# Two-layer encoder on one core: other distances in SBUF between the weight tiles and the activation parts

## The chip, the core and the metric

The kernel runs on one core of a Trainium2 chip. Its engines are TensorE (PE, with its weight loads shown apart as PEld), VectorE (DVE), ScalarE (ACT), GpSimd (POOL) and SyncE (SP, which only issues DMAs here). The metric is device time in microseconds of one execution.

## What is computed

An encoder trunk of two layers on 256 tokens of width 1024, all in float32. Each layer is a SwiGLU half-step, a mixer with 16 attention heads, a second SwiGLU half-step and a gate:

```
for i in range(2):
    x = x + 0.5 * swiglu(rms_norm(x, norm_ffn1[i]), ffn1_w_in[i], ffn1_w_out[i])   # 1024 -> 2 x 2816 -> 1024
    h = rms_norm(x, norm_mix[i])
    qa, ka, va, qb, kb, vb = split(h @ w_qkv[i])                 # 8 heads A, 8 query and 2 key heads B, 64 wide
    oa = dilated_attention(norm(qa), norm(ka), va, bias_a)
    ob = banded_attention(norm(qb), norm(kb), vb, 128, bias_b, sink_b[i])
    x = x + concat(oa, ob) @ w_o[i]
    x = x + 0.5 * swiglu(rms_norm(x, norm_ffn2[i]), ffn2_w_in[i], ffn2_w_out[i])
    x = x + sigmoid(rms_norm(x, norm_ple[i]) @ w_ple_gate[i]) * (p[i] @ w_ple_proj[i])
```

## The kernel before, in words

Every float32 operand of a matrix product is split into two parts of type float32r, an upper (h) and a lower (l), and a product is three matmuls into one PSUM bank: upper by upper, upper by lower, lower by upper (`mm3`). The stationary operand (lhsT, loaded into the array) is a 128 x 128 tile of the transposed activations; the moving operand (rhs, streamed through it) is 512 or 256 columns of a weight tile.

The weights come as chunks of 128 x 1024 floats, in one fixed order (class `Weights`). SP's queue loads a chunk into one of four `wraw` buffers; ScalarE writes its upper part `whi`, VectorE its lower part `wlo`, eight buffers each. The next load is issued when a `wraw` buffer is free again.

The activations' parts are: `ah`, `al`, x^T in two parts for each token tile of 128, made by `x_T` for an `Acts` object, one object a stage; they are the stationary operand of the products with w_in, w_qkv and the gate's weights. `pth`, `ptl`, three buffers each from `take_pt`: in a half-step h^T, the transposed block j of 256 hidden columns (11 blocks a half-step), the stationary operand of the product with w_out (`unit_rows`); in the mixer the transposed probabilities, there the moving operand of the product with v. `oth`, `otl`: the heads' outputs and p^T in the mixer, and x^T of the first half-step of all (`first_acts`). Transposes are matmuls with an identity, through the banks `tp` and `op`.

Class `Pace` keeps an expected clock and from it fixes the order in which the program issues instructions on each engine. Addresses don't enter into it.

Tiles lie in SBUF in the order of the pools. Of the start of each tile in a partition the build gives, in bytes past a multiple of 512:

| tile | before | after |
|---|---|---|
| whi, wlo (all buffers; every slice used starts a multiple of 1024 further on) | 480 | 0 |
| ah, al | 480 | 0 plus the stage's shift |
| pth, ptl in the half-steps | 32 | 0 plus the block's shift |
| oth, otl | 32 | 0 |
| qah, qal, kah, kal, qbh, qbl, kbh, kbl | 32 | 0 |
| vah, val, vbh, vbl | 480 | 0 |
| identity | 96 | 128 |

All buffers of one name have the same remainder, and the 128 stationary columns used at a time (512 bytes) begin at multiples of 512 from the tile's start; those of v begin at multiples of 256. So each product has one distance, start of the stationary slice minus start of the weight slice, mod 512: before, 0 for ah and al with whi and wlo, and 64 for pth, ptl, oth and otl with them. For q k it is 0, for the product with v 192 or 448.

Of the kernel before, what the change touches and what calls it, by code (L numbers as in the profile page):

```python
# [32 lines left out]
def shape_constants():  # L33
    """One-hot T5 buckets and additive log-multiplicity masks by position distance 255 - i."""
    d = 255 - np.arange(512)
    n = np.abs(d)
    half, exact = NB // 2, NB // 4
    nf = np.maximum(n, 1).astype(np.float32)
    large = exact + (
        np.log(nf / np.float32(exact)) / np.float32(math.log(MAXD / exact)) * np.float32(half - exact)  # L40
    ).astype(np.int32)
    large = np.minimum(large, half - 1)
    bucket = np.where(d > 0, half, 0) + np.where(n < exact, n, large)
    onehot = (np.arange(NB)[:, None] == bucket[None, :]).astype(np.float32)
    mult = (n <= 64).astype(int) + (d % 4 == 0) + (d % 16 == 0)
    mask_a = np.where(mult > 0, np.log(np.maximum(mult, 1)), NEG)
    mask_b = np.where(n <= 128, 0.0, NEG)
    masks = np.stack([mask_a, mask_b]).astype(np.float32)
    sel = np.zeros((2, NHA + NHB), np.float32)
    sel[0, :NHA] = 1.0  # L50
    sel[1, NHA:] = 1.0
    return onehot, masks, sel
# [5 lines left out]
def column_chunks(w, starts, width):  # L58
    """[D, 1024, N] to chunks [D, starts, chunk, 128, 1024]: the columns from starts on, by feature rows."""
    blocks = [np.concatenate([w[:, :, c:c + width] for c in cols], axis=2) for cols in starts]  # L60
    v = np.stack(blocks, axis=1)
    cw = v.shape[-1]
    v = v.reshape(DEPTH, len(starts), KD * cw // 1024, 1024 // cw, 128, cw)
    return np.ascontiguousarray(v.transpose(0, 1, 2, 4, 3, 5)).reshape(DEPTH, len(starts), -1, 128, 1024)


def lay_out(inputs):
    """The inputs as the kernel loads them: contiguous chunks, token-transposed copies, gains by partition."""
    a = {name: np.ascontiguousarray(v) for name, v in inputs.items()}
    onehot, masks, sel = shape_constants()  # L70
    d = {}
    for name in ("ffn1", "ffn2"):
        starts = [(j * FB, DFF + j * FB) for j in range(NFB)]
        d[name + "_in"] = column_chunks(a[name + "_w_in"], starts, FB)
        d[name + "_out"] = a[name + "_w_out"].reshape(DEPTH, -1, 128, DM)
    d["qkv"] = np.concatenate([column_chunks(a["w_qkv"], [(c0,)], cw)[:, 0] for _, c0, cw in QKV_BLOCKS], axis=1)
    for name, w in (("wo", "w_o"), ("gate", "w_ple_gate"), ("ple", "w_ple_proj")):
        d[name] = a[w].reshape(DEPTH, -1, 128, DM)
    x = a["x"][0].reshape(2, 128, DM)
    d["x"] = x  # L80
    d["xT"] = a["x"][0].T.reshape(4, 2, 128, S).transpose(0, 2, 1, 3)
    d["pT"] = a["p"][:, 0].reshape(DEPTH, S, 2, 128).transpose(0, 3, 2, 1)
    g = [a[n].reshape(DEPTH * KD, 128) for n in ("norm_ffn1", "norm_mix", "norm_ffn2", "norm_ple")]
    g += [np.concatenate([a[n], a[n]], axis=1) for n in ("q_norm_a", "k_norm_a", "q_norm_b", "k_norm_b")]
    d["gains"] = np.concatenate(g).T
    d["sink"] = a["sink_b"].reshape(1, -1)
    d["bias"] = np.concatenate([a["rel_bias"], sel])
    d["distance"] = np.concatenate([onehot, masks])
    return {name: np.ascontiguousarray(v) for name, v in d.items()}


# The start: identities that keep the tensor engine busy, and when the first loads are expected.
# [6 lines left out]
class Pace:  # L99
    """The order in which instructions are issued.  # L100

    Each engine runs its instructions in the order of issue. The tensor engine is the
    busiest, so its expected progress is the clock: work for the other engines is issued
    once what it needs is expected to be there, and never ahead of work that can go first.
    """
# [12 lines left out]
    def done(self):  # L118
        """When the other engines can see what the tensor engine has been given so far."""
        return self.now + self.FROM_PE  # L120
# [13 lines left out]
    def at(self, t, fn, engine=None, prio=0):  # L134
        """fn() from time t on; with an engine: once that is free, the lowest prio first."""
# [3 lines left out]
    def check(self):  # L139
        """Issues what has become due, then weight splitting into the time that is left."""  # L140
# [16 lines left out]
    def until(self, cond):  # L157
        """Nothing else is left for the tensor engine: waits for an event's result."""
# [6 lines left out]
class Weights:  # L165
    """The stream of weight chunks, each [128, 1024] columns, split into two float32r parts.

    Chunks are loaded, split and used in one fixed order; a chunk's slots are free again
    once it has had all its uses.
    """  # L170
# [12 lines left out]
    def add(self, src, pieces, uses=2):  # L183
        """src: [128, 1024] in DRAM; pieces: (start, stop, gain or None)."""
# [16 lines left out]
    def ready(self):  # L201
        """When the next chunk has arrived and its slots are free."""
        return max(self.arrived.get((self.cut, self.at), self.arrived[self.cut]), self.freed.get(self.cut - self.SPLIT, 0.0))

    def piece(self):
        """Up to 512 columns: the upper part now, the lower part when that is expected."""
# [35 lines left out]
    def lows(self, n):  # L242
        """Issues the lower parts up to the n-th; loads what can go into the raw slots then free."""
# [9 lines left out]
    def pump(self):  # L253
        """Splits ahead while the engines for it have nothing more urgent."""
# [27 lines left out]
def encoder(ctx: ExitStack, tc, ins, out):  # L282
# [16 lines left out]
    # A slot is taken again only when all that uses it has been issued: a total order, no deadlock.  # L299
# [16 lines left out]
    def give(tile, t=0.0):  # L316
        """tile's slot can be taken from time t on; all that uses tile has been issued."""
        kind, k, _ = owner.pop(id(tile))
        slots[kind][k] = t
# [8 lines left out]
    def when(kind, fn):  # L328
        """fn() once a slot can be taken."""
# [11 lines left out]
    W = Weights(nc, pace, wraw_p, whi_p, wlo_p)  # L341
    pace.fill = W.pump
    gains = const.tile([P, 72], F32, name="gains")
# [46 lines left out]
    def unit_cols(ps, a, t, ids, c, cw, kks=None):  # L390
        """ps += chunk c's part of the product with token tile t."""
# [13 lines left out]
    def unit_rows(acc, ah, al, c, first, last, ready):  # L405
        """acc[n] += (ah + al)^T (row chunk c) for the two column halves n."""
# [8 lines left out]
    def transposes(kind, blocks, ready=0.0):  # L415
        """blocks: (destination columns / 128, source); on a bank of its own."""
# [7 lines left out]
    def with_bank(kind, t, fn):  # L424
        """fn() from time t on, once the transposes' bank is expected to be free."""
# [7 lines left out]
    def parts(hi, lo, src, n, scale=None, bank=None, then=None, ready=None, prio=1):  # L433
        """hi + lo = src * scale; returns when they are expected. bank: src's, free after that."""
# [28 lines left out]
    x_sb = const.tile([P, 2, DM], F32, name="x_sb")  # L463
    xT_in = [tile_L() for _ in range(4)]
# [25 lines left out]
    # The tensor engine's clock rises once it has been busy: identities until the first data is there.  # L490
# [5 lines left out]
    def setup():  # L496
        """The scales of q k^T, and the position bias by distance, one DRAM row per head."""
# [11 lines left out]
        nc.gpsimd.dma_start(out=bias_d, in_=bs[:16, :])  # L509
        give(bs)  # L510

    # v with zero columns beside it, so that a head's product fills its half of a pair's rows
# [15 lines left out]
    class Acts:  # L528
        def __init__(self, hi=None, lo=None):
            def part(name, given):  # L530
                if given is not None:
                    return [given[:, :, t * P:(t + 1) * P] for t in range(2)]
                return [act_p.tile([P, KD, P], F32R, tag=f"{name}{t}", name=f"{name}{t}") for t in range(2)]
# [5 lines left out]
    def x_T(a, t, ready):  # L539
        """Issues x^T of token tile t when x is expected, each half as soon as it can."""  # L540
# [10 lines left out]
    def stats(a, t):  # L551
        """1/rms of token tile t's rows."""
# [24 lines left out]
    def first_acts():  # L577
        """The parts of x^T and of the first weights, in the order of their loads."""
# [22 lines left out]
    def take_pt():  # L601
        return take("pt", *(att.tile([P, 2, S], F32R, tag=g, name=g, bufs=3) for g in ("pth", "ptl")))
# [6 lines left out]
    def ffn(a, ids, first=False):  # L609
# [27 lines left out]
        def h_T(j, ts, ready):  # L637
            if j not in hT:
                hT[j] = take_pt()
# [73 lines left out]
    def mixers(i, a, d):  # L713
# [13 lines left out]
        def head_T(key, ps, t, nh, perm, scale, dst):  # L727
            """Normed heads, two by two transposed into dst: hi and lo [2 heads' features, pairs, tokens]."""
# [56 lines left out]
        def block(name, kind, cw, evac, split=False):  # L785
            """A generator of the block's units, with evac(ps, t) after a token tile's last."""
# [41 lines left out]
        def qk(h):  # L828
# [23 lines left out]
            def logits():  # L852
                """L = -(q k + bias), nm = -max, or -max with the sink."""
# [79 lines left out]
        def embed():  # L933
            """The two parts of this layer's p^T; they lie where later heads' outputs will."""
            pr = ple[1][:, 512:]
            nc.gpsimd.dma_start(out=pr.rearrange("q (k c) -> q k c", k=2), in_=ins["pT"][i])
# [4 lines left out]
        def ple_unit(t, n):  # L941
            """A quarter of p W_ple."""
# [85 lines left out]
    def gate(a, ids, ple, final):  # L1028
# [3 lines left out]
        def unit(k, t, some=None):  # L1032
            """Adds feature tile k to token tile t's column groups."""
# [81 lines left out]
```

## Time and profile before

| | |
|---|---|
| time, median of 2 runs | 1053.22 us (1052.98 to 1053.46) |
| span of the profiled execution, first to last instruction | 1051.8 us |
| TensorE busy | 1044.9 us, 99% of the span |
| VectorE, ScalarE busy | 686.5 us, 640.5 us |
| matmuls | 4978, as many weight loads |
| granted clock of TensorE | 1.000 in the mean |

The records of matmuls overlap: one starts while the one before is still in the array. So the busy time and the mean duration of a group don't tell what a matmul costs a busy TensorE; the distance from one start to the next does, and that is read from the timeline.

### The profile page before, as it was taken

To read this page: it belongs to the slowest core of one execution; us is meant where nothing else is said; L and a number is where in the kernel's file an instruction comes from. 1 tells how busy PE (TensorE), PEld (TensorE's weight loads), DVE (VectorE), ACT (ScalarE), POOL (GpSimd) and SP (SyncE) were. 2 spreads that over 40 slices of the span, in tenths; PEclk is the share of its full clock that TensorE was granted. 3 is DMA by queue.
4 is the path that set the end of the run, shared out by engine and by line. 5 is a ranking of instruction groups with operands and counts; after the bars stand their busy time and mean duration, and the time that the engine had idled before them with its cause. 6 is when DMAs were issued, how large, how long until landed. Compare 5 with 4: busy or idle time off the path is not lost.

```text
span 1051.8 us, 14143 instructions
## 1 busy us (share of the span) xinstructions
PE 1044.9 (99%) x4978; PEld 859.1 (82%) x4978; DVE 686.5 (65%) x1286; ACT 640.5 (61%) x1222; POOL 35.9 (3%) x41
## 2 busy tenths in 40 slices
PE   9999999999999999999999999999999999999998
PEld 7788888888888888888887888888888888888887
DVE  6765554787887555555676555557878875555654
ACT  7755454667787555554785555556677865555553
POOL 0000000120100000000000000002110000000000
PEclk9999999999999999999999999999999999999999
DMA  8765554464446555555456555544634465555531
GB/s 310 251 224 181 181 180 160 143 217 134 144 150 201 185 181 193 186 182 173 166 173 208 193 187 181 186 168 148 217 108 146 141 221 189 188 183 184 188 130 41
DMA packets 55774, 187.19 MB, mean 178 GB/s; under 512 B 6502, under 2 KB 10854, under 8 KB 55704
## 3 DMA queue, kind: packets, MB, share of 16 engines
q1 hardware_dynamic: 55512, 185.74, 52.5%
q8 instruction: 39, 0.64, 0.2%
q0 software_dynamic: 192, 0.56, 0.2%
q14 instruction: 31, 0.25, 0.1%
HBM read 185.19 MB, written 1.08 MB: 177 GB/s over the span
## 4 chain that ended last, share of the span: by engine, by line
PE 98%; DMA 1%; DVE 1%; ACT 0%; issue 0%; SPq 0%; ACTq 0%
PE mm L382 52%; PE acc L382 38%; PE tp L419 4%; PE op L382 2%; PE op L419 1%; DMA wraw<-in_ffn_out_dram 1%; DMA wraw<-in_ffn_in_dram 0%; DVE wlo L227 0%; PE mm L419 0%; PE acc L419 0%; DVE wlo L229 0%; ACT whi L220 0%; PE op L504 0%; ACT sq L617 0%; DVE L L623 0%
## 5 line engine op out<-in xcount | busy, mean ns | idle before, releaser
L229 DVE SCALAR_TENSOR_TENSOR wlo<-wraw,gains,whi 128x512 fp32r<-128x512 f32 (+1 forms) x464 | 322.4, 738 | 142.8 <-ACT whi L222 137.1
L222 ACT ACTIVATE whi<-wraw,gains 128x512 fp32r<-128x512 f32 (+1 forms) x464 | 306.0, 709 | 147.2 <-PE mm L382 91.0
L382 PE MATMUL mm<-whi,ah 128*128 128x512 f32 (+1 forms) x632 | 248.6, 393 | 0.0
L382 PE MATMUL mm<-whi,al 128*128 128x512 f32 (+1 forms) x632 | 245.7, 389 | 0.0
L382 PE MATMUL mm<-wlo,ah 128*128 128x512 f32 (+1 forms) x632 | 245.5, 388 | 0.0
L220 ACT CAST whi<-wraw 128x512 fp32r<-128x512 f32 x216 | 126.3, 617 | 84.9 <-PE mm L382 74.0
L227 DVE TENSOR_TENSOR wlo<-wraw,whi 128x512 fp32r<-128x512 f32 x216 | 139.9, 686 | 47.4 <-ACT whi L220 47.1
L382 PE MATMUL acc<-whi,pth 128*128 128x512 f32 x352 | 143.1, 406 | 0.0
L382 PEld LDWEIGHTS mm<-whi,ah 128*128 128x128 f32 x632 | 118.7, 188 | 25.2
L382 PE MATMUL acc<-whi,ptl 128*128 128x512 f32 x352 | 139.2, 396 | 0.0
L382 PEld LDWEIGHTS mm<-whi,al 128*128 128x128 f32 x632 | 118.7, 188 | 24.9
L382 PE MATMUL acc<-wlo,pth 128*128 128x512 f32 x352 | 139.0, 395 | 0.0
L382 PEld LDWEIGHTS mm<-wlo,ah 128*128 128x128 f32 x632 | 118.8, 188 | 23.7
L623 DVE SCALAR_TENSOR_TENSOR L<-mm,r,sq 128x256 f32<-128x256 f32 x86 | 41.6, 484 | 68.6 <-ACT sq L617 68.4
L382 PEld LDWEIGHTS acc<-whi,ptl 128*128 128x128 f32 x352 | 66.3, 188 | 16.1
L382 PEld LDWEIGHTS acc<-wlo,pth 128*128 128x128 f32 x352 | 66.3, 188 | 13.7
L382 PEld LDWEIGHTS acc<-whi,pth 128*128 128x128 f32 x352 | 66.2, 188 | 13.5
L439 ACT CAST pth<-tp 128x512 fp32r<-128x512 f32 (+1 forms) x70 | 39.2, 560 | 49.7 <-PE tp L419 49.6
L447 DVE TENSOR_TENSOR ptl<-tp,pth 128x512 fp32r<-128x512 f32 (+1 forms) x70 | 46.2, 659 | 32.3 <-ACT pth L439 32.3
L382 PE MATMUL mm<-whi,oth 128*128 128x512 f32 x160 | 63.4, 396 | 0.0
L382 PE MATMUL mm<-wlo,oth 128*128 128x512 f32 x160 | 63.2, 395 | 0.0
L382 PE MATMUL mm<-whi,otl 128*128 128x512 f32 x160 | 63.2, 395 | 0.0
(136 smaller groups left out, 1196.7 us busy)
## 6 DMA issues: line engine op xcount, KB each, us to landing
wraw<-in_ffn_in_dram SPq DMA_DIRECT2D x172, 512.0 KB, 3.3
wraw<-in_ffn_out_dram SPq DMA_DIRECT2D x88, 512.0 KB, 3.3
wraw<-in_qkv_dram SPq DMA_DIRECT2D x36, 512.0 KB, 3.3
wraw<-in_wo_dram SPq DMA_DIRECT2D x16, 512.0 KB, 3.5
wraw<-in_gate_dram SPq DMA_DIRECT2D x16, 512.0 KB, 3.2
bias<-bias_d SPq DMA_DIRECT2D x32, 192.0 KB, 3.5
wraw<-in_ffn_in_dram SPq DMA_DIRECT2D x8, 256.0 KB, 5.6
wraw<-in_ple_dram SPq DMA_DIRECT2D x4, 512.0 KB, 3.3
```

The source lines that it names most:

```text
L220: nc.scalar.copy(hi[:, a:b], raw[:, a:b])
L222: nc.scalar.activation(hi[:, a:b], raw[:, a:b], AF.Copy, scale=g)
L227: nc.vector.tensor_tensor(out=lo[:, a:b], in0=raw[:, a:b], in1=hi[:, a:b].bitcast(F32), op=ALU.subtract)
L229: nc.vector.scalar_tensor_tensor(out=lo[:, a:b], in0=raw[:, a:b], scalar=g, in1=hi[:, a:b].bitcast(F32), op0=ALU.mult, op1=ALU.subtract)
L382: nc.tensor.matmul(ps, lhsT=lhsT, rhs=rhs, start=start, stop=stop)
L419: nc.tensor.transpose(tp[:, n * P:(n + 1) * P], src, ident)
L439: nc.scalar.copy(hi, src)
L447: nc.vector.tensor_tensor(out=lo, in0=src, in1=hi.bitcast(F32), op=ALU.subtract)
L623: nc.vector.scalar_tensor_tensor(out=hs[j][:, t, :], in0=ps[:, FB:], scalar=a.r[t], in1=s, op0=ALU.mult, op1=ALU.mult)
```

## The change

Weight tiles and the pools behind them begin at multiples of 512 bytes: `gains` is given eight more floats and an unused tile `align` of 448 bytes stands in the pool `sm`. The parts of x^T and h^T get 128 floats more room (`shifted`), and start at a shift inside it. For x^T the shift is taken from `X_AT` by stage, in floats; object 0 (`first_acts`) lies in oth and otl and has none. For h^T it goes up by four floats, 16 bytes, with each column block of the four half-steps, and starts again after 32. In the mixer `take_pt` has shift 0. In bytes:

| stage | shift = distance from the weight tile |
|---|---|
| layer 1: ffn1 (oth, otl) | 0 |
| layer 1: mixer, ffn2, gate | 16, 32, 256 |
| layer 2: ffn1, mixer, ffn2, gate | 48, 128, 64, 384 |
| h^T, blocks 0 to 43 over the four half-steps | 0, 16, 32, ..., 496, 0, ..., 176 |
| w_o and p W_ple (oth, otl) | 0 |

[...] Comments are left out of the file, so its lines have other numbers.

```diff
-    gains = const.tile([P, 72], F32, name="gains")
+    gains_t = const.tile([P, 80], F32, name="gains")
+    gains = gains_t[:, :72]
...
     x_sb = const.tile([P, 2, DM], F32, name="x_sb")
+    sm.tile([P, 112], F32, tag="align", name="align", bufs=1)
...
-        nc.gpsimd.dma_start(out=bias_d, in_=bs[:16, :])
+        nc.sync.dma_start(out=bias_d, in_=bs[:16, :])
...
+    stage = [0]
+    X_AT = (0, 4, 8, 64, 12, 32, 16, 96)
+    SLACK = 128
+
+    def shifted(pool, tag, n, at, shape, bufs):
+        t = pool.tile([P, n + SLACK], F32R, tag=tag, name=tag, bufs=bufs)
+        return t[:, at:at + n].rearrange(shape[0], **shape[1])
+
     class Acts:
         def __init__(self, hi=None, lo=None):
+            at = X_AT[stage[0]]
+            stage[0] += 1
+
             def part(name, given):
                 if given is not None:
                     return [given[:, :, t * P:(t + 1) * P] for t in range(2)]
-                return [act_p.tile([P, KD, P], F32R, tag=f"{name}{t}", name=f"{name}{t}") for t in range(2)]
+                return [shifted(act_p, f"{name}{t}", KD * P, at, ("p (k q) -> p k q", {"k": KD}), 1) for t in range(2)]
...
-    def take_pt():
-        return take("pt", *(att.tile([P, 2, S], F32R, tag=g, name=g, bufs=3) for g in ("pth", "ptl")))
+    def take_pt(at=0):
+        return take("pt", *(shifted(att, g, 2 * S, at, ("p (k q) -> p k q", {"k": 2}), 3) for g in ("pth", "ptl")))
...
+    h_at = [0]
...
-                hT[j] = take_pt()
+                hT[j] = take_pt(4 * h_at[0])
+                h_at[0] = (h_at[0] + 1) % 32
...
-            nc.gpsimd.dma_start(out=pr.rearrange("q (k c) -> q k c", k=2), in_=ins["pT"][i])
+            nc.sync.dma_start(out=pr.rearrange("q (k c) -> q k c", k=2), in_=ins["pT"][i])
...
-    nc = bacc.Bacc("TRN2", target_bir_lowering=False, num_devices=1)
+    nc = bacc.Bacc("TRN2", target_bir_lowering=False, num_devices=1, dynamic_dma_scratch_size=4096)
```

On TensorE, ScalarE and VectorE the instructions and their order stay as they are. On SP's queue three DMAs are added. The first place is in the first half-step, at the loads for column blocks 1 and 2 (names in brackets are the semaphores waited for: DMAHW of earlier DMAs, DVE of VectorE). Before:

```order
L193 DMA wraw<-in_ffn_in_dram 128x1024 [waits DMAHW7_49,DVE_49]
L193 DMA wraw<-in_ffn_out_dram 128x1024 [waits DMAHW4_49,DMAHW0_49,DVE_49]
L193 DMA wraw<-in_ffn_out_dram 128x1024 [waits DMAHW5_49,DMAHW1_49,DVE_49]
L193 DMA wraw<-in_ffn_in_dram 128x1024 [waits DMAHW6_49,DMAHW2_49,DVE_49]
L193 DMA wraw<-in_ffn_in_dram 128x1024 [waits DMAHW3_49,DVE_49]
```

And now:

```order
L193 DMA wraw<-in_ffn_in_dram 128x1024 [waits DMAHW7_49,DVE_49]
L193 DMA wraw<-in_ffn_out_dram 128x1024 [waits DMAHW4_49,DMAHW0_49,DVE_49]
L511 DMA bias_d<-sq 16x512 [waits DMAHW5_49,DVE_49]
L193 DMA wraw<-in_ffn_out_dram 128x1024 [waits DMAHW6_49,DMAHW1_49,DVE_49]
L193 DMA wraw<-in_ffn_in_dram 128x1024 [waits DMAHW2_49,DVE_49]
```

The write of bias_d stands between the two loads of a pair of w_out chunks and waits for VectorE's copy into sq. The second place is on SP in the first layer's mixer, among the loads of w_o and of the heads' bias tiles. Before:

```order
L193 DMA wraw<-in_wo_dram 128x1024 [waits DMAHW4_49,DVE_49]
L710 DMA bias<-bias_d 128x384
L710 DMA bias<-bias_d 128x384 [waits DMAHW6_49,DVE_49]
L193 DMA wraw<-in_wo_dram 128x1024 [waits DMAHW5_49,DVE_49,Activation_49]
L710 DMA bias<-bias_d 128x384 [waits DMAHW1_49]
```

And now:

```order
L193 DMA wraw<-in_wo_dram 128x1024 [waits DMAHW5_49,DVE_49]
L727 DMA bias<-bias_d 128x384
L953 DMA ple<-in_pT_dram 128x512
L727 DMA bias<-bias_d 128x384 [waits DMAHW7_49,DMAHW6_49,DVE_49]
L193 DMA wraw<-in_wo_dram 128x1024 [waits DVE_49,Activation_49]
L727 DMA bias<-bias_d 128x384 [waits DMAHW2_49,DMAHW0_49]
```

The load of p^T stands between two bias tiles and waits for nothing; in the second layer it is the same.

## Rows read from the trace of the kernel before

**Rows 1.** The page's head: span; busy time, share and instructions of each engine; the granted clock in 40 slices.

```profile
span 1051.8 us, 14143 instructions
...
PE 1044.9 (99%) x4978; PEld 859.1 (82%) x4978; DVE 686.5 (65%) x1286; ACT 640.5 (61%) x1222; POOL 35.9 (3%) x41
...
PEclk9999999999999999999999999999999999999999
```

**Rows 2.** The page's chain that ended last, by engine.

```profile
PE 98%; DMA 1%; DVE 1%; ACT 0%; issue 0%; SPq 0%; ACTq 0%
```

**Rows 3.** Groups of TensorE's instructions by form, whole span (line, engine, operation, out<-in, rows*columns of the stationary tile, shape of the output, count | busy us, mean ns of one | idle before).

```profile
L382 PE MATMUL mm<-whi,ah 128*128 128x512 f32 x624 | 246.4, 395 | 0.0
...
L382 PE MATMUL acc<-whi,pth 128*128 128x512 f32 x352 | 143.1, 406 | 0.0
...
L382 PE MATMUL mm<-whi,oth 128*128 128x512 f32 x160 | 63.4, 396 | 0.0
...
L382 PE MATMUL acc<-whi,oth 128*128 128x512 f32 x96 | 40.5, 422 | 0.2 <-ACT whi L222 0.2
...
L382 PE MATMUL acc<-whi,ah 128*128 128x512 f32 x88 | 35.1, 399 | 0.0
...
L382 PE MATMUL acc<-whi,ah 128*128 128x256 f32 x40 | 11.8, 296 | 0.0
...
L382 PE MATMUL acc<-kah,qah 64*128 64x256 f32 x32 | 10.5, 330 | 0.0
...
L382 PE MATMUL op<-pth,vah 128*128 128x256 f32 x32 | 8.4, 285 | 0.0
...
L382 PE MATMUL mm<-whi,ah 128*128 128x256 f32 x8 | 2.3, 283 | 0.0
```

**Rows 4.** Timeline of TensorE, 415 to 426.4 us, in the second half-step of the first layer: start us, duration us, engine, line, operation, out<-in. The first and the last of 41 matmuls on x^T in a row, then the nine on h^T behind them.

```profile
415.02 0.39 PE L382 MATMUL mm<-wlo,ah 128*128 128x512 f32 x1
415.25 0.39 PE L382 MATMUL mm<-whi,al 128*128 128x512 f32 x1
...
424.09 0.39 PE L382 MATMUL mm<-whi,al 128*128 128x512 f32 x1
424.32 0.40 PE L382 MATMUL acc<-whi,pth 128*128 128x512 f32 x1
424.55 0.39 PE L382 MATMUL acc<-wlo,pth 128*128 128x512 f32 x1
...
426.18 0.40 PE L382 MATMUL acc<-whi,ptl 128*128 128x512 f32 x1
```

**Rows 5.** Timeline of TensorE in the first half-step, 36.6 to 46.3 us: the first two and the last of 41 matmuls on oth and otl in a row.

```profile
36.69 0.39 PE L382 MATMUL mm<-whi,oth 128*128 128x512 f32 x1
36.93 0.39 PE L382 MATMUL mm<-wlo,oth 128*128 128x512 f32 x1
...
46.03 0.39 PE L382 MATMUL mm<-wlo,oth 128*128 128x512 f32 x1
```

**Rows 6.** Timeline of a matmul and of the weight load beside it, in the stretch of rows 4.

```profile
416.16 0.39 PE L382 MATMUL mm<-whi,ah 128*128 128x512 f32 x1
...
416.16 0.19 PEld L382 LDWEIGHTS mm<-wlo,ah 128*128 128x128 f32 x1
```

**Rows 7.** Timeline of TensorE in the first layer's mixer: matmuls of 256 columns, on x^T (distance 0), with v (448), and with v again (192).

```profile
242.36 0.28 PE L382 MATMUL acc<-wlo,ah 128*128 128x256 f32 x1
...
243.20 0.28 PE L382 MATMUL acc<-whi,al 128*128 128x256 f32 x1
243.32 0.28 PE L382 MATMUL op<-pth,vah 128*128 128x256 f32 x1
243.44 0.28 PE L382 MATMUL op<-pth,val 128*128 128x256 f32 x1
...
243.79 0.40 PE L382 MATMUL op<-ptl,vah 128*128 128x256 f32 x2
...
247.25 0.28 PE L382 MATMUL op<-pth,vah 128*128 128x256 f32 x1
...
247.49 0.40 PE L382 MATMUL op<-ptl,vah 128*128 128x256 f32 x2
```

**Rows 8.** Timeline of SP's queue (duration of a merged row: from its first issue to the end of its last), of VectorE's copy and of GpSimd's issues; and the tile view of bias_d, with the duration of SP's issues of bias tiles in ns, min/median/max.

```profile
30.96 4.19 SPq L193 DMA_DIRECT2D wraw<-in_ffn_out_dram  x2
36.15 0.33 SPq L193 DMA_DIRECT2D wraw<-in_ffn_in_dram  x1
...
240.02 3.00 SPq L710 DMA_DIRECT2D bias<-bias_d  x2
249.20 0.33 SPq L193 DMA_DIRECT2D wraw<-in_wo_dram  x1
...
32.80 0.68 DVE L507 COPY sq<-op 16x512 f32<-16x512 f32 x1 [1.25 <-PE op L504]
...
33.78 0.68 POOL L509 DMA_DIRECT2D bias_d<-sq  x1 [12.17 <-DVE sq L507]
...
245.62 0.60 POOL L936 DMA_DIRECT2D ple<-in_pT_dram  x1
...
L710 SPq DMA_DIRECT2D bias<-bias_d x32: 319/408/767, 218.2 to 810.7; - x32
```

## Prediction

> **What bounds the kernel now.** [...] No wait is worth removing: only what a matmul takes of TensorE's time can move the end. The change alters no instruction on TensorE, ScalarE or VectorE, so all of it stands or falls with the spacing of matmuls, from the start of one to the start of the next.
>
> The groups by form give the counts [rows 3]; each row is one of three passes with the same count. With 512 columns there are 3 x (624 + 88) = 2136 matmuls on x^T (ah, al), 3 x 352 = 1056 on h^T (pth, ptl), and 3 x (160 + 96) = 768 on oth/otl: 3960 in all. The group means (395 against 406 ns) are durations that overlap and can't be summed; the timeline gives the spacing. On x^T 40 matmuls take 424.09 - 415.02 = 9.07 us, 226.7 ns each; on h^T eight take 426.18 - 424.32 = 1.86 us, 233 ns each [rows 4]; on oth/otl forty take 46.03 - 36.69 = 9.34 us, 233.4 ns [rows 5]. [...]
>
> Which operand makes the difference? All three use the same whi and wlo, and x^T and h^T stand side by side in one stage. What differs is where the stationary operand lies: 0 bytes from the weight tile, mod 512, for x^T, 64 for both others. A weight load starts together with a matmul and is over before the next, 0.19 us in a slot of 0.23 [rows 6], so the two reads lie beside each other in time. I take the spacing as a function of that distance, with two values known: 226.7 at 0, 233.3 at 64.
>
> **The change part by part.** *oth/otl* go from 64 to 0: 768 x (226.7 - 233.3) = -5.1 us.
>
> *x^T* goes from 0 to one distance per stage. Per half-step 528 matmuls have 512 columns, per mixer 192, 96 and 72 in the gates. At 64 (second layer's ffn2) there is a row: 528 x 6.6 = +3.5 us. At 16, 32, 48, 128, 256 and 384, with 192 + 528 + 528 + 192 + 96 + 72 = 1608 matmuls, there is none for 512 columns. [...] For a distance without a row I take the mean of four losses, 13.4 at 0, 20 at 64 and 11.3 at 192 and at 448, which is 14.0: a spacing of 227.3. That costs 1608 x 0.6 = +1.0 us; the ends are 224.6 (-3.4 us) and 233.3 (+10.6 us). I take the mean and not a line from 0 to 64, since nothing shows that the function is smooth.
>
> *h^T* goes from 64 to 0, 16, ..., 496 over 44 column blocks of 24 matmuls; the first twelve distances come twice. At 227.3: 1056 x (227.3 - 233.3) = -6.3 us; ends -9.2 us (all 224.6) and 0 (all 233.3).
>
> *The weight tiles* start at 0 instead of 480 bytes past a multiple of 512. No row has a matmul with another start: every tile that TensorE streams begins 32 bytes past a multiple of 64. [...]
>
> *Matmuls of 256 columns and transposes*: q k stays at 0, the products with v go from 192 and 448 to 0 and 256. Between 118 and 120 ns this is at most 192 x 2 ns = 0.4 us: zero.
>
> *Three DMAs go from POOL's queue to SP's.* bias_d waits for VectorE's copy, which ends at 32.80 + 0.68 = 33.48 us. On SP it stands between two issues of ffn_out chunks, whose pair takes from 30.96 to 35.15 us; the second is 0.33 long like the single issues, so it starts near 34.8 [rows 8]. The copy is done 1.3 us earlier, SP is idle, and the chunk behind is not held back. An issue on SP takes 0.32 to 0.77 us, as those of bias do [rows 8], still inside the gap. p^T falls between SP's issues that end at 243.02 and start at 249.20 [rows 8], where POOL issued it at 245.62; it has no wait of its own. If SP were not idle there, a chunk would come under 1 us later, against a lead of four chunks. Zero, and no engine but TensorE can become the bound through a few per cent less TensorE time: VectorE is at 65%, ScalarE at 61% [rows 1].
>
> Sum: -5.1 + 3.5 + 1.0 - 6.3 = -6.9 us, so a span of 1044.9. The runs' median, 1053.2, lies 1.4 us over the profiled span, so 1046.3.
>
> [...]
>
> **The rivals.**
>
> [...]
>
> *2. 0 is the good distance and the rest are like 64* (slower). Place: x^T, the largest group, is moved away from 0. All 2136 at 233.3 cost +14.1 us, h^T gains only its two blocks at 0 (48 x 6.6 = 0.3 us), oth/otl 5.1: +8.7, so 1062. It decides as soon as the mean over x^T's distances exceeds 226.7 + (5.1 + 6.3) / 2.136 = 232.0 ns with h^T at its mean; over 2% it needs distances worse than 64. For it: the only nonzero distance with 512 columns is the slow one. Against it: 192 and 448 are no slower than 0 at 256 columns.
>
> *3. Distance does nothing* and 226.7 against 233 comes from something else in the stages: 1053. Against it: in one stage, with the same engines beside it, the spacing steps within one matmul or a few of the change of tile [rows 4].
>
> **How the numbers follow.** Forecast 0.45, its own range 1039 (both low ends: -3.4 + 3.5 - 9.2 - 5.1 = -14.2) to 1056 (x^T at its high end, +9.6 on the forecast). Rival 1: 0.30, at 1016, spread by the same unknowns from 1008 to 1030. Rival 2: 0.17, 1056 to 1072. Rival 3: 0.08. I predict the likeliest, 1046 us. The range 1010 to 1062 leaves out a small part of rival 1 and half of rival 2 at most, under 0.15. Faster by over 2% is under 1032, which is all but a little of rival 1 and a small tail of the forecast: 0.32. Slower by over 2% is over 1074: a tail of rival 2, 0.04. Within 2%, about what a measurement of this kernel can tell from no change: 0.64.
>
> **What would show it.** [...] SP's issues near 33.5 and 243 us show the moved DMAs, and no wait of ScalarE on wraw should follow them. The forecast is wrong if the function has deep valleys or peaks where half-steps lie, 32 and 48 above all: 10 ns at either is 5.3 us.

## The result and the profile after

| | before | after |
|---|---|---|
| time, median | 1053.22 us (1052.98 to 1053.46) | 1058.54 us (1058.34 to 1058.74) |
| span of the profiled execution | 1051.8 us | 1056.9 us |

The ratio is 1.0052, interval 1.0033 to 1.0071: slower by half a per cent, within 2%, but with the interval clear of 1. The forecast was 1046, faster by 0.7%.

The page of the kernel after: span, TensorE's busy time, the chain that ended last.

```profile
span 1056.9 us, 14146 instructions
...
PE 1050.4 (99%) x4978; PEld 860.5 (81%) x4978; DVE 687.5 (65%) x1286; ACT 640.4 (61%) x1222; POOL 34.6 (3%) x38
...
PE 97%; DMA 1%; DVE 1%; ACT 0%; issue 0%; SPq 0%; ACTq 0%; DVEq 0%
```

Against [rows 1, 2] the bound is the same, and TensorE's busy time has grown by 5.5 us, the span by 5.1. So the change in time must lie in the spacing of matmuls, from the start of one to the start of the next. The timeline of TensorE after, start us and duration us first: the first two and the last of 44 matmuls on oth and otl at distance 0, from the stretch of [rows 5]; then of the second half-step nine matmuls on h^T at 192, nine at 240, 48 on x^T at 32 (three rows), and nine on h^T at 256.

```profile
36.23 0.39 PE L383 MATMUL mm<-whi,oth 128*128 128x512 f32 x1
36.46 0.39 PE L383 MATMUL mm<-wlo,oth 128*128 128x512 f32 x1
...
45.98 0.39 PE L383 MATMUL mm<-wlo,oth 128*128 128x512 f32 x1
...
354.59 0.39 PE L383 MATMUL acc<-whi,pth 128*128 128x512 f32 x1
...
356.42 0.39 PE L383 MATMUL acc<-whi,ptl 128*128 128x512 f32 x1
...
406.17 0.39 PE L383 MATMUL acc<-whi,pth 128*128 128x512 f32 x1
...
408.00 0.39 PE L383 MATMUL acc<-whi,ptl 128*128 128x512 f32 x1
...
412.10 0.39 PE L383 MATMUL mm<-whi,ah 128*128 128x512 f32 x1
412.33 0.39 PE L383 MATMUL mm<-wlo,ah 128*128 128x512 f32 x1
...
423.06 0.40 PE L383 MATMUL mm<-whi,al 128*128 128x512 f32 x1
423.29 0.39 PE L383 MATMUL acc<-whi,pth 128*128 128x512 f32 x1
...
425.11 0.39 PE L383 MATMUL acc<-whi,ptl 128*128 128x512 f32 x1
```

oth and otl went from 233.4 [rows 5] to (45.98 - 36.23) / 43 = 226.7 ns. x^T at 32 went from 226.7 [rows 4] to (423.06 - 412.10) / 47 = 233.2. These nine matmuls on h^T stand at 229 (192), 229 (240) and 228 (256); the other fifteen of each block, behind the next break (other matmuls in between), settle at 229, 226.7 and 226.7.

Each matmul's distance to the next start, summed over the whole trace and grouped by operand and stage, gives the balance in us:

| 512 columns | count | before | after | measured | forecast |
|---|---|---|---|---|---|
| oth, otl, 64 to 0 | 768 | 182.8 | 179.2 | -3.6 | -5.1 |
| x^T to 64 (layer 2, ffn2) | 528 | 120.3 | 123.4 | +3.1 | +3.5 |
| x^T to 32, 48 (ffn2, then ffn1) | 1056 | 240.8 | 246.9 | +6.1 | +0.6 |
| x^T to 16, 128 (mixers) | 384 | 91.2 | 92.2 | +1.1 | +0.2 |
| x^T to 256, 384 (gates) | 168 | 38.7 | 39.0 | +0.3 | +0.1 |
| h^T, 64 to all distances | 1056 | 250.2 | 248.8 | -1.4 | -6.3 |
| all other matmuls (256 columns, transposes) | 1018 | 121.5 | 121.3 | -0.2 | 0 |

The differences are taken before rounding. Their sum is +5.4 us against +5.1 of the spans; the stretch behind the last matmul became 0.2 us shorter. For x^T the forecast took 0.6 ns a matmul, except at 64, where it had a row.

### The profile page after: what moved, and what is told of

Same layout as the page of the kernel before. It is cut to its first block, busy times and chain, and to the rows that moved or that the text cites. A ratio compares the mean times of both kernels' runs of the same rounds, so it can differ in the third digit from the quotient of the medians.

```text
span 1056.9 us, 14146 instructions
## 1 busy us (share of the span) xinstructions
PE 1050.4 (99%) x4978; PEld 860.5 (81%) x4978; DVE 687.5 (65%) x1286; ACT 640.4 (61%) x1222; POOL 34.6 (3%) x38
## 4 chain that ended last, share of the span: by engine, by line
PE 97%; DMA 1%; DVE 1%; ACT 0%; issue 0%; SPq 0%; ACTq 0%; DVEq 0%
PE mm L383 52%; PE acc L383 38%; PE tp L420 4%; PE op L383 2%; DMA wraw<-in_ffn_in_dram 1%; DVE wlo L229 1%; PE op L420 1%; PE mm L420 0%; ACT whi L222 0%; PE acc L420 0%; PE op L506 0%; ACT val L522 0%; ACT vbh L522 0%; DVE ptl L448 0%; DVE L L639 0%
## 5 line engine op out<-in xcount | busy, mean ns | idle before, releaser
L383 PE MATMUL mm<-whi,ah 128*128 128x512 f32 (+1 forms) x632 | 252.0, 399 | 0.0
L383 PE MATMUL mm<-whi,al 128*128 128x512 f32 (+1 forms) x632 | 249.0, 394 | 0.0
L383 PE MATMUL mm<-wlo,ah 128*128 128x512 f32 (+1 forms) x632 | 249.0, 394 | 0.0
L383 PEld LDWEIGHTS acc<-whi,pth 128*128 128x128 f32 x352 | 66.3, 188 | 13.4
L633 ACT ACTIVATE sq<-mm,r 128x256 f32<-128x256 f32 x86 | 40.5, 472 | 36.6 <-PE mm L383 36.3
```

The source lines that it names most:

```text
L383: nc.tensor.matmul(ps, lhsT=lhsT, rhs=rhs, start=start, stop=stop)
L633: nc.scalar.activation(s, ps[:, :FB], AF.Silu, scale=a.r[t])
```

## The experiments

Theory after the result: the spacing hangs on the distance between the two tiles of a product; 0 is among the few good values, and 64 and most other multiples of 16 are bad. Rivals: the start of the streamed tile alone, the start of the stationary tile alone, the DMAs moved to SP, and the distance between a weight load and the slice streamed beside it, which belongs to the matmul before (the two start together, at 416.16 us in [rows 6]). Beside all of these but the last the kernel before took 1053.39 to 1053.48 us.

**All at 0, on the kernel after.**

```diff
-    X_AT = (0, 4, 8, 64, 12, 32, 16, 96)
+    X_AT = (0,) * 8
...
-                hT[j] = take_pt(4 * h_at[0])
+                hT[j] = take_pt(0)
```

> The changed kernel with every shift 0: x^T, h^T, oth and otl all at distance 0. Theory 1 (the spacing goes by the distance between the stationary slice and the weight slice; 0 is a good distance, 226.7 ns): x^T back to the spacing of before, h^T and oth/otl at 227 to 228, so 1043 to 1044 us, about 10 us under before. Theory 2 (the loss of the change comes from the three DMAs on SP's queue or from the new starts of the tiles, not from distances): it stays near 1058.

Measured 1044.14 us, ratio 0.9913 (0.9899 to 0.9926), span 1042.3. Its timeline, 48 matmuls on x^T and the nine on h^T behind them:

```profile
408.29 0.39 PE L383 MATMUL mm<-whi,ah 128*128 128x512 f32 x1
...
418.94 0.39 PE L383 MATMUL mm<-whi,al 128*128 128x512 f32 x1
419.17 0.39 PE L383 MATMUL acc<-whi,pth 128*128 128x512 f32 x1
...
420.98 0.39 PE L383 MATMUL acc<-whi,ptl 128*128 128x512 f32 x1
```

They run at 10.65 / 47 = 226.6 and 1.81 / 8 = 226 ns. So the rest of the change costs nothing, and all of its loss lies in the distances.

**All at 0, on the kernel before.** One unused tile moves pth, ptl, oth and otl to 480; the weight tiles stay at 480 too.

```diff
     x_sb = const.tile([P, 2, DM], F32, name="x_sb")
+    sm.tile([P, 112], F32, tag="align", name="align", bufs=1)
```

> The kernel before with one unused tile of 448 bytes ahead of the attention pool, so that h^T, oth and otl come to distance 0; the weight tiles stay at 480 bytes past a multiple of 512, the DMAs stay on POOL. Theory 1: the same 1043 to 1044 us as with all shifts 0. If the start of the weight tiles at a multiple of 512 is worth something by itself: slower than that run.

Measured 1044.43 us, 0.9917 (0.9903 to 0.993). It equals the version with weight tiles at multiples of 512 to 0.3 us: where the streamed tile starts is worth nothing, and one line beats both kernels.

**Half of it: x^T at 0, h^T at its 32 distances.** X_AT is zero in the kernel after, take_pt as it was.

> The changed kernel with x^T's shifts alone set to 0, h^T's distances as in the change. Theory 1: x^T wins back its 10.4 us, so 1048 us. Theory 2: near 1058.

Measured 1047.42 us, 0.9945 (0.9932 to 0.9957). Of the 14.4 us between after and all at 0, x^T holds 11.1, h^T 3.3.

**The DMAs alone, on the kernel before.**

```diff
-        nc.gpsimd.dma_start(out=bias_d, in_=bs[:16, :])
+        nc.sync.dma_start(out=bias_d, in_=bs[:16, :])
...
-            nc.gpsimd.dma_start(out=pr.rearrange("q (k c) -> q k c", k=2), in_=ins["pT"][i])
+            nc.sync.dma_start(out=pr.rearrange("q (k c) -> q k c", k=2), in_=ins["pT"][i])
```

> The kernel before with its three GpSimd DMAs issued by SP, no tile moved. Theory 1: 1053 us, no change. Theory 2: up to 1058.

Measured 1053.38 us, 1.0001 (0.9992 to 1.001). In the kernel after, which has the same DMAs on SP: SP's queue in the stretches of [rows 8], in the first half-step and the first mixer, and VectorE's copy:

```profile
30.67 0.33 SPq L193 DMA_DIRECT2D wraw<-in_ffn_out_dram  x1
33.11 0.33 SPq L511 DMA_DIRECT2D bias_d<-sq  x1
34.44 0.33 SPq L193 DMA_DIRECT2D wraw<-in_ffn_out_dram  x1
...
237.46 0.43 SPq L727 DMA_DIRECT2D bias<-bias_d  x1
237.94 0.43 SPq L953 DMA_DIRECT2D ple<-in_pT_dram  x1
240.12 0.33 SPq L727 DMA_DIRECT2D bias<-bias_d  x1
...
32.41 0.68 DVE L509 COPY sq<-op 16x512 f32<-16x512 f32 x1 [1.15 <-PE op L506]
```

The write of bias_d goes out at the end of the copy (33.09), and SP is idle for 1.0 us before the chunk behind. p^T goes out between two bias tiles, and SP is idle for over 1.7 us behind it.

**Difference or start?** The version at 0, but weight tiles and x^T both start 64 bytes past a multiple of 512, so that x^T's distance is still 0, and that of h^T, oth and otl, which stay, 448. (h^T's tiles also lose their 128 floats of room, with no shift to use it.)

```diff
-            hi = self.hi_pool.tile([128, 1024], F32R, tag="whi", name="whi")
-            lo = self.lo_pool.tile([128, 1024], F32R, tag="wlo", name="wlo")
+            hi = self.hi_pool.tile([128, 1152], F32R, tag="whi", name="whi")[:, 16:1040]
+            lo = self.lo_pool.tile([128, 1152], F32R, tag="wlo", name="wlo")[:, 16:1040]
...
-    X_AT = (0,) * 8
+    X_AT = (16,) * 8
```

> All shifts 0, then the weight tiles and x^T both 64 bytes further on: x^T is at distance 0 but starts 64 bytes past a multiple of 512; h^T, oth and otl start at 0 and lie at distance 448 (192 mod 256). If the difference of the two starts decides: x^T at 227 to 228 ns, the other two at the 229 ns that h^T's block at 448 showed, 1046 to 1047 us. If the start of the stationary slice alone decides (0 good, 64 bad): x^T at 233, the others at 227, about 1052 us.

Measured 1046.52 us, 0.9932 (0.9917 to 0.9947). Of its timeline, the second and the last of 48 matmuls on oth and otl at 448, then 48 on x^T at 0:

```profile
36.21 0.39 PE L383 MATMUL mm<-wlo,oth 128*128 128x512 f32 x1
...
46.74 0.39 PE L383 MATMUL mm<-whi,otl 128*128 128x512 f32 x1
...
375.56 0.39 PE L383 MATMUL mm<-whi,ah 128*128 128x512 f32 x1
...
386.22 0.39 PE L383 MATMUL mm<-whi,al 128*128 128x512 f32 x1
```

x^T runs at 10.66 / 47 = 226.8 ns, oth and otl at 10.53 / 46 = 228.9. A stationary start at 64 with the stream's start at 64 is as good as 0 with 0 (226.8 ns here, 226.6 there), so the start of the stationary tile alone doesn't decide. 229 at 448 is what h^T takes at 192 in the kernel after.

**Steps of 4 bytes, for h^T, then for x^T.** In the version with x^T at 0, `take_pt(48 + h_at[0])` gives h^T 192, 196, ..., 316. Then, with h^T at 0, X_AT = (0, 62, 1, 56, 2, 63, 60, 48), that is 248, 4, 224, 8, 252, 240, 192 bytes.

> x^T, oth and otl at 0; h^T's blocks at distances 192, 196, ..., 316 in steps of 4 bytes. If distances within one 16-byte line are alike, blocks change in groups of four: 229 at 192 to 204, 233 at 208 to 236, 227 to 228 at 240 to 268, 233 from 272 or 288. If the good distances are single points, 256 alone is at 227. No distance under 226.7 is expected. Time near 1046 us.

> All shifts 0 but x^T's: half-steps at 4, 8 and 240 bytes (528 matmuls each), mixers at 248 and 252, gates at 224 and 192. From h^T's blocks: 240 at 227, 192 at 229, 224 at 233; 4, 8, 248 and 252 have short blocks that lay between 229 and 233. If distances inside one 16-byte line are alike, 4 and 8 are at 227.

Measured 1047.64 and 1051.87 us, one run each. Of the first, nine matmuls on h^T at 252 behind a stream at distance 0, and then the fourteen behind a break:

```profile
403.54 0.39 PE L383 MATMUL acc<-whi,pth 128*128 128x512 f32 x1
...
405.35 0.39 PE L383 MATMUL acc<-whi,ptl 128*128 128x512 f32 x1
...
406.26 0.40 PE L383 MATMUL acc<-wlo,pth 128*128 128x512 f32 x1
...
409.29 0.40 PE L383 MATMUL acc<-whi,ptl 128*128 128x512 f32 x1
```

Of the second, 48 on x^T at 4, and 48 at 240:

```profile
342.72 0.39 PE L383 MATMUL mm<-whi,ah 128*128 128x512 f32 x1
...
353.65 0.39 PE L383 MATMUL mm<-whi,al 128*128 128x512 f32 x1
...
864.85 0.39 PE L383 MATMUL mm<-whi,ah 128*128 128x512 f32 x1
...
875.50 0.39 PE L383 MATMUL mm<-whi,al 128*128 128x512 f32 x1
```

At 4 it is 10.93 / 47 = 232.6 ns: four bytes off 0 cost nearly all. At 240 it is 226.6, at 8 230.7. So distances within 16 bytes of each other aren't alike. And at 252 one and the same distance shows two spacings, 1.81 / 8 = 226 and 3.03 / 13 = 233 ns. So the distance alone doesn't settle it, which the last kernel below takes up.

**One of the two parts moved by 64 bytes**, on the version at 0: first `al`, then `ah`, in all stages that have x^T in them.

```diff
-                return [shifted(act_p, f"{name}{t}", KD * P, at, ("p (k q) -> p k q", {"k": KD}), 1) for t in range(2)]
+                return [shifted(act_p, f"{name}{t}", KD * P, at + 16 * (name == "al"), ("p (k q) -> p k q", {"k": KD}), 1) for t in range(2)]
```

> All shifts 0, but al alone at distance 64: of the three loads of a group, ah, ah, al, one is at 64. If each load at 64 costs its 6.7 ns in the slot beside it: 712 x 6.7 = 4.7 us less what refills hide, 1047 to 1049 us, and the long slot is that of wlo on ah, beside which al is loaded. If the rhythm of the whole group changes at once: 1044 (stays at 226.7) or 1052 (all at 233.3).

> All shifts 0, but ah alone at distance 64: two of three loads at 64. If each load at 64 costs 6.7 ns: 1424 x 6.7 = 9.5 us at most, 1051 to 1053 us. If the rhythm of the whole group changes at once: 1044 or 1052.

Measured 1052.07 us, 0.9989 (0.998 to 0.9999), and 1055.47 us, 1.002 (1.001 to 1.0029); all at 0 was 1044.14. Of the timelines, 48 matmuls with al moved, then in a second fence with ah moved:

```profile
359.19 0.39 PE L383 MATMUL mm<-whi,ah 128*128 128x512 f32 x1
...
370.05 0.40 PE L383 MATMUL mm<-whi,al 128*128 128x512 f32 x1
```

```profile
359.26 0.40 PE L383 MATMUL mm<-whi,ah 128*128 128x512 f32 x1
...
370.22 0.39 PE L383 MATMUL mm<-whi,al 128*128 128x512 f32 x1
```

They run at 10.86 / 47 = 231.1 and 10.96 / 47 = 233.2 ns. Neither expectation held: the 1052 us given for the first agrees in number only, since it stood for a spacing of 233.3. With al moved only one product in three is at 64, and yet a group of three takes 13 ns more (693 against 680 at 0), twice the 6.6 between 233.3 and 226.7; with ah moved it takes 20 more in the half-steps (700). Nor is the long slot the one that was expected: with al moved it is that of whi on al, 235.9 ns in the mean against 228.3 and 229.1 for the other two, and not that of wlo on ah, beside which al is loaded. The cost isn't additive over the products: a group of three changes its rhythm together.

**A load and the slice streamed beside it.** On the version at 0: wlo, al, ptl and otl moved by 64 bytes, so that each weight load is at distance 0 from the slice streamed while it runs, and the products' own distances are 0, 448 and 64; and wlo alone moved by 128.

```diff
-            lo = self.lo_pool.tile([128, 1024], F32R, tag="wlo", name="wlo")
+            lo = self.lo_pool.tile([128, 1152], F32R, tag="wlo", name="wlo")[:, 16:1040]
...
-        lo = att.tile([P, KD, S], F32R, tag="otl", name="otl")
+        lo = shifted(att, "otl", KD * S, 16, ("p (k q) -> p k q", {"k": KD}), 1)
```

(otl in both places where it is made, and 16 floats for al and ptl in the same way; the second kernel has `[:, 32:1056]` for wlo and no other edit)

> All shifts 0, then wlo, al, ptl and otl 64 bytes further on. A group of three streams whi, wlo, whi; beside them the loads are of the upper part, the lower part and the next upper part, at 0 - 0, 64 - 64 and 0 - 0: each load lies at 0 from the slice streamed beside it, while a matmul's own two operands lie at 0, 448 and 64. If the load and the stream beside it decide: 226.7 ns throughout, 1044 us. If a matmul's own operands decide, or the starts alone: 231 to 233 ns, 1052 to 1056 us.

> All shifts 0, then wlo alone 128 bytes further on, so that beside its stream the lower part is loaded from 384 (128 mod 256), one load of three at a bad distance and all stationary starts at 0. If the load and the stream beside it decide: as with al alone at 64, 231 ns in the mean; there x^T alone cost 8 us, here h^T, oth and otl too (3960 matmuls instead of 2136), 1044 + 8 x 3960 / 2136 = 1059 us. If the starts of the stationary slices decide: 1044 us.

Measured 1056.34 us, 1.0029 (1.0018 to 1.004), and 1063.06 us, 1.0092 (1.0075 to 1.0109). In steady stretches the first runs at 231 ns on x^T and h^T and 233 on oth and otl, the second at 233 on all. A distance of 0 to the slice beside the load isn't enough, and with stationary starts as in the best version wlo alone costs 18.9 us: the start of one tile relative to the other decides. The distance beside the load alone fails at the first of these, and a price for each product by its own distance, added up, fails at the kernels with al, ah or wlo moved. That one product's distance sets the rhythm of its whole group isn't excluded. In both kernels h^T is moved too, so they don't tell what a stream at 226.7 ahead of x^T would have done.

**Two rhythms?** On the version at 0, X_AT = (0, 0, 63, 0, 74, 0, 67, 0): x^T at 252, 296 and 268, three of the distances that showed two spacings.

> The version with everything at distance 0, but x^T at 252 in the first layer's second half-step, at 296 in the second layer's first and at 268 in its second. In the run with h^T in steps of 4 bytes these three distances showed two spacings: nine matmuls that came straight out of a stream at 226.7 ns stayed at 226.6, and the fourteen behind the next break ran at 233.6, 233.5 and 229.6. Theory that there are two rhythms there, and that a stream keeps the one it enters with: the long runs of 48 x^T matmuls that follow h^T at 227 stay at 227, and only the runs behind transposes at a half-step's start are at 233, some 135 of 528: 3 x 135 x 6.6 ns = 2.7 us over 1044.1, so 1047. Rival, that nine matmuls are too few to settle and the distance alone decides in the end: the 48 drift to 233 and all 1584 cost 6.6 ns, less at 268: 1052 to 1054.5.

Measured 1045.07 us, with 1053.82 for the kernel before beside it, one run each. In its timeline, x^T at 252: 47 matmuls behind the transposes that begin the half-step, then 48 behind h^T at distance 0.

```profile
314.41 0.40 PE L383 MATMUL mm<-wlo,ah 128*128 128x512 f32 x1
...
325.15 0.39 PE L383 MATMUL mm<-whi,al 128*128 128x512 f32 x1
...
341.52 0.39 PE L383 MATMUL mm<-whi,ah 128*128 128x512 f32 x1
...
352.18 0.39 PE L383 MATMUL mm<-whi,al 128*128 128x512 f32 x1
```

The same tiles in the same half-step: 10.74 / 46 = 233.5 ns in the first run, 10.66 / 47 = 226.8 in the second, and 226.7 in each later run of 48 of the three half-steps. The theory of two rhythms holds, and the drift that its rival expected isn't there; the time came out 2 us under the 1047 expected, since the three half-steps cost only +0.2 to +0.6 us each over distance 0: 108 of the 528 matmuls ran slower behind breaks and not 135, those at 268 at 230 ns only, and at distance 0 the first matmuls behind a break are slow too (231 ns in the mean of nine).

## Why the prediction was wrong

**What bounds the kernel, and which operand decides.** Right. TensorE is busy 99% of the span before [rows 1] and after, and nothing but the spacing moved the time, x^T in the half-steps and oth/otl changed places at 226.7 and 233.3, the two known values, and the two kernels with all at 0 are 9.0 and 9.3 us under the kernel before. Rival 3 falls: all at 0 took 1044.14 us and the kernel after 1058.54, with only starts of tiles different.

**The step that failed** is "For a distance without a row I take the mean of four losses". Its losses of 13.4, 20 and 11.3 ns are counted from a spacing without loss that was the author's assumption; no run shows it, and the 227.3 and the low end of 224.6 rest on it. At distance 0 the rows show 226.7 ns for 512 columns and 120.0 for 256 [rows 4, 7], and no steady stretch of 512 columns ran under 226 in any run. Two of the four came from matmuls of 256 columns at 192 and 448, and these are one case, not two: what the runs show repeats every 256 bytes (0 and 256: 226.7 and 227; 192 and 448: 229 at both; 176 and 432: 230 at both, steady stretches of h^T after). Nor does what they show hold for 512 columns: at 448 and 192 five matmuls of 256 take 0.35 + 0.24 us, 118 ns each and 2 under the 120 at distance 0 [rows 7], while 512 columns take 229 there, 2 over the 226.7 at distance 0. So a difference read at 256 columns doesn't carry over to 512. And even so 192 is one of the few better values, with 0, 240 and 176: of h^T's thirty-two distances after, 23 have means of 232 to 235, and x^T's half-steps sit on three of these. So the x^T stages off 64 cost +7.5 us, where the step gave +1.0, and h^T won 1.4, where it gave 6.3. The text named 32 and 48 as the places that could undo it, and both are among the 23. Their timeline in the kernel after, at 48 and at 64:

```profile
558.04 0.40 PE L383 MATMUL mm<-whi,ah 128*128 128x512 f32 x1
...
569.01 0.39 PE L383 MATMUL mm<-whi,al 128*128 128x512 f32 x1
...
867.43 0.40 PE L383 MATMUL mm<-whi,ah 128*128 128x512 f32 x1
...
878.40 0.39 PE L383 MATMUL mm<-whi,al 128*128 128x512 f32 x1
```

10.97 / 47 = 233.4 ns at either. Rival 2, "0 is the good distance and the rest are like 64", was right in kind; its 1062 is 3.5 us high, mostly because it prices x^T's small stages in full too (all of x^T +14.1, measured +10.6).

**A premise below that step.** "I take the spacing as a function of that distance" holds for 0 (it settles at 226.7 whatever came before) and for 4, 32, 48, 64 (232 to 233.4 whatever came before), but not everywhere: at 16, 252, 268, 272 and 296 a stream that comes in at 226.7 ns keeps it, and otherwise, or behind a break, it can run at 230 to 233.5. The kernel after shows it too, on x^T at 16 in the first mixer, 41 matmuls and then 32 behind a break:

```profile
197.84 0.39 PE L383 MATMUL mm<-wlo,ah 128*128 128x512 f32 x1
...
206.92 0.40 PE L383 MATMUL mm<-whi,al 128*128 128x512 f32 x1
...
207.82 0.40 PE L383 MATMUL acc<-wlo,ah 128*128 128x512 f32 x1
...
215.06 0.40 PE L383 MATMUL acc<-whi,al 128*128 128x512 f32 x1
```

9.08 / 40 = 227 ns, then 7.24 / 31 = 233.5. And h^T at 272 has two spacings though its own tiles are the same: nine matmuls in the kernel with x^T alone at 0, behind x^T at 226.7, and in a second fence in the kernel after, behind x^T at 233.

```profile
436.96 0.39 PE L383 MATMUL acc<-whi,pth 128*128 128x512 f32 x1
...
438.77 0.39 PE L383 MATMUL acc<-whi,ptl 128*128 128x512 f32 x1
```

```profile
440.44 0.40 PE L383 MATMUL acc<-whi,pth 128*128 128x512 f32 x1
...
442.30 0.40 PE L383 MATMUL acc<-whi,ptl 128*128 128x512 f32 x1
```

1.81 / 8 = 226 ns and 1.86 / 8 = 233.

**Terms that were mis-sized.** oth/otl: -5.1 forecast, -3.6 measured; x^T at 64: +3.5 and +3.1. The 6.6 ns a matmul is won only in steady stretches: behind a break, such as the transposes, the nine matmuls after the first take 231 ns in the mean at distance 0 as well (68 breaks of the kernel with all at 0). For the same cause h^T at 0 throughout won 4.7 us there (250.2 - 245.4) and not 1056 x 6.6 ns = 7.0.

**Terms at nothing.** The start of the weight tiles: nothing (1044.14 against 1044.43). Rival 1, at 1016, gave the start of the streamed tile a price of its own; no run shows one, and it falls. 256 columns and transposes: -0.2 us. The DMAs: nothing. bias_d went out at the place and for the reason given; p^T didn't go out between 243.02 and 249.20 us, where the text put it, but between two bias tiles, whose issues [rows 8] shows merged in one row. SP was idle there too.

## What to carry to other kernels

Where TensorE is the bound and streams matmuls with a weight load each, read the start-to-start spacing by operand and set it beside the starts of both tiles in their partitions: here one unused tile that puts every product with a weight tile at distance 0 won 0.8%. Keep a distance known to be good: a spread over others isn't a neutral average, since here most of them are bad (23 of 32 at 232 to 235 ns, against 226.7 at 0). Of a function with two known values, don't fill the rest with a mean: say which untested points the time hangs on, and give the case "all like the bad one" a larger share.

## What the runs showed of the hardware

- Matmuls of 512 columns with a weight load each run in steady stretches mostly at one of two spacings, 226.7 or 233.3 ns. Between them lie 229 (at 192), 230 (at 176) and, with al alone moved by 64 bytes, 231 (693 ns a group of three). The spacing depends on the two tiles' starts relative to each other (x^T at 64 with the weight tiles at 64: 226.8), repeats every 256 bytes (0 and 256: 226.7 and 227; 192 and 448: 229; 176 and 432: 230), and is as fine as 4 bytes (0: 226.7, 4: 232.6, 8: 230.7, 240: 226.7, 248: 233.3).
- At some distances there are two steady rhythms, and a break in the stream or what runs before it picks one (252: 226.8 or 233.5 in one half-step; 272: 226 or 233 by the stream ahead).
- Where the weight tiles start, past a multiple of 512 or of 64, doesn't matter by itself (0.3 us of 1044).
- Open: what in the chip makes it. Neither the distance to the slice beside the load nor an added price for each product's own distance gives all the times, and no run here took the weight loads away from the streams.
